# First mixer: the second group's keys between turning the first head's weights and their use; two splits of weights moved behind the first S5 outputs

## The chip, the cores and the metric

The kernel runs as one program on one core of a Trainium2 chip. The metric is the device time of one execution in microseconds (us); the time before is the median of three executions. The engines are PE (matrix products and transposes), ACT and DVE (elementwise work), POOL (a little elementwise work) and SP (it issues the transfers of weights). Each runs its own list of instructions, and semaphores tie the lists together.

## What is computed

A decoder trunk of two layers on 256 tokens of width 1024, all in float32. Each layer is half a SwiGLU block, a mixer, and half a SwiGLU block. The change lies in the mixer of the first layer, which joins a diagonal state space model (S5) and latent attention (MLA):

```python
def _even_mixer(h, ...):
    u, c_q, c_kv, k_rope = jnp.split(h @ w_in, ...)          # 512, 384, 256, 32 columns
    s5_out = _s5(u, ...)                                     # scan over time, gelu, GLU
    q = (_rmsnorm(c_q, q_norm) @ w_uq)                       # 8 heads of 64 + 32 (rotated)
    kv = (_rmsnorm(c_kv, kv_norm) @ w_ukv)                   # 8 heads: keys of 64, values of 64
    ...
    o = _causal_attention(q_full, k_full, v)                 # 8 heads, 256 x 256, blocks of 128 rows
    return jnp.concatenate([s5_out, o], axis=-1) @ w_out
```

## The kernel before

Every product with weights is made of three products of rounded parts: a piece of float32 weights (128x1024, 512 KB) is loaded into one of five `stage` buffers, ACT casts it into `whi` (L84), and DVE subtracts to get the rest, `wlo` (L85). Cast and subtraction together are a split. After each piece's split the next load is issued on SP's queue (`self.load(1)`), so loads run five pieces ahead of splits. In a mixer the call `more()` splits the next chunk of weights, two pieces as a rule, into a pair of buffers; two such pairs exist, and `queue` holds the chunks that are ready.

In the first mixer MLA's eight heads form two groups of four (g = 0, 1). `queries(g)` (L942) and `keys(g)` (L954) fill `qk`, the queries and keys of four heads; `key_values(g)` (L965) fills `v_sb`. For one head `scores(h)` makes a product `sp` (L1045, L1046), DVE takes the row maxima (L831, two blocks of rows) and ACT the exponentials (L838). `turned` transposes these weights on PE (`pt`, L844), and ACT copies them to `pT` (L846); `values` (L1059 to L1061) multiplies them with `v_sb` into `po`. `attend(h)` turns the weights of head h+1, makes the scores of head h+3, and then the values of head h.

S5 works on two halves (b = 0, 1). `step(b)` lets DVE do the next part of the states of half b: products with cosines and sines, two scans (L990), and then `xs_re` and `xs_im`, each of two multiplications and one subtraction or addition (all through the helper at L144). `outputs(b)` (L1086 to L1088) is 48 PE products per half, eight times two passes each of `tmat`, `xs_re` and `xs_im` into `yp`.

The program is written out by hand as a sequence of such calls at the end of `mixer0`. The tile framework puts the instructions of each engine into an order of its own, near that of the code; each engine then takes its list in that order. Shown in the order of the code, the stretch that matters is:

```python
        queries(1)
        step(0)
        sc[0] = turned(sc[0], pb)
        attend(0)
        step(1)
        keys(1)
        key_values(1)
        attend(1)
        step(1)
        yp = outputs(0)
        attend(2)
```

At the end of `queries(1)` a `more()` splits the output weights `w_out0[2]`, and at the end of `key_values(1)` one splits `w_glu`.

Of the kernel before, what the change touches and what calls it, by code (L numbers as in the profile page):

```python
# [99 lines left out]
def highs_first(ks, whi, wlo, xhi, xlo):  # L100

    ks = list(ks)
    return [(k, w, xhi) for k in ks for w in (whi, wlo)] + [(k, whi, xlo) for k in ks]
# [3 lines left out]
def trunk(ctx: ExitStack, tc: tile.TileContext, x, pos, invf, wff, gains, w_u, w_cq, w_ckv,  # L107
# [16 lines left out]
    def bank(name):  # L124
        return ps.tile([128, 512], F32, tag="bank", name=name)
# [16 lines left out]
    def tt(out, a, b, op):  # L142
        spend(out)
        return nc.vector.tensor_tensor(out=out, in0=a, in1=b, op=op)  # L144
# [696 lines left out]
    def turned(s, pool_):  # L841
        pt = bank("pt")
        for c in range(3):
            nc.tensor.transpose(pt[:, c * 128:(c + 1) * 128], s[:, c * 128:(c + 1) * 128], ident)  # L844
        pT = pool_.tile([128, 384], F32, tag="pT", name="pT")
        nc.scalar.copy(out=pT, in_=pt[:, :384])  # L846
        return pT


    def mixer0(prev):  # L850
# [3 lines left out]
        def more():  # L854
            queue.append(W.pre())
# [76 lines left out]
            for g in range(2):  # L932
                nc.scalar.copy(out=kT[64:, 4 * g:4 * g + 4, :], in_=pt[64:].unsqueeze(1).to_broadcast([64, 4, SEQ]))

        def queries(g, between=None):

            wh, wl = (w[:, :1536].rearrange("p (k h d) -> p k h d", k=3, h=4) for w in queue.pop(0))
            for b in range(2):
                pq = bank("pq").rearrange("p (h c) -> p h c", h=2)
                for j in range(2):  # L940
                    for n, (k, w, a) in enumerate(highs_first(range(3), wh, wl, cqh, cql)):
                        nc.tensor.matmul(pq[:, j], w[:, k, 2 * b + j], a[:, k, :], start=n == 0, stop=n == 8)  # L942
                h = 4 * g + 2 * b
                tt(qT[:, h:h + 2, :], pq, qtab.unsqueeze(1).to_broadcast([128, 2, SEQ]), MUL)
                if b == 0 and between:
                    between()
            more()

        def keys(g):
            wh, wl = (w[:, :1024].rearrange("p (k s c) -> p k s c", k=2, s=2) for w in queue[0])  # L950
            pk = bank("pk").rearrange("p (j c) -> p j c", j=2)
            for j in range(2):
                for n, (k, w, a) in enumerate(highs_first(range(2), wh, wl, ckh, ckl)):
                    nc.tensor.matmul(pk[:, j], w[:, k, 0, 128 * j:128 * j + 128], a[:, k, :], start=n == 0,  # L954
                                     stop=n == 5)
            for r in range(2):
                nc.scalar.copy(out=kT[:64, 4 * g + r:4 * g + 4:2, :], in_=pk[64 * r:64 * r + 64])

        def key_values(g):
            wh, wl = (w[:, :1024].rearrange("p (k s c) -> p k s c", k=2, s=2) for w in queue.pop(0))  # L960
            pv = bank("pv").rearrange("p (t c) -> p t c", t=2)
            for t in range(2):
                sl = slice(t * 128, (t + 1) * 128)
                for n, (k, w, a) in enumerate(highs_first(range(2), wh, wl, ckh, ckl)):
                    nc.tensor.matmul(pv[:, t], a[:, k, sl], w[:, k, 1, :], start=n == 0, stop=n == 5)  # L965
            nc.scalar.copy(out=v_sb[:, :, 256 * g:256 * g + 256], in_=pv)
            more()

        xs_re, xs_im = s4("xs_re", [128, NPAIR, NBLK]), s4("xs_im", [128, NPAIR, NBLK])
        nc.gpsimd.memset(xs_re[:, :, 0:1], 0.0)  # L970
# [40 lines left out]
        def step(b):  # L1011
            next(st[b], None)
# [21 lines left out]
        pb = att.enter_context(tc.tile_pool(name="att2", bufs=2))  # L1034
# [8 lines left out]
        def scores(h):  # L1043
            sp = bank("sp")
            nc.tensor.matmul(sp[:, :128], qT[:, h, :128], kT[:, h, :128], start=True, stop=True)  # L1045
            nc.tensor.matmul(sp[:, 128:384], qT[:, h, 128:], kT[:, h, :], start=True, stop=True)  # L1046
            s = pa.tile([128, 384], F32, tag="s", name="s")
            mx = small("mx2", 2)
            row_maxima(sp, s, 96 ** -0.5, mx)
            row_exps(s, mx, lsum[:, 2 * h:2 * h + 2])  # L1050
            return s

        def values(h, pT):
            g, k = divmod(h, 4)
            if k == 0:
                po[g] = bank("po").rearrange("p (t h d) -> p t h d", t=2, h=4)
            o = po[g]
            v = slice(64 * h, 64 * h + 64)
            nc.tensor.matmul(o[:, 0, k, :], pT[:, :128], v_sb[:, 0, v], start=True, stop=True)  # L1059
            nc.tensor.matmul(o[:, 1, k, :], pT[:, 128:256], v_sb[:, 0, v], start=True, stop=False)  # L1060
            nc.tensor.matmul(o[:, 1, k, :], pT[:, 256:384], v_sb[:, 1, v], start=False, stop=True)  # L1061
# [20 lines left out]
        def outputs(b):  # L1082
            yp = bank("yp").rearrange("p (q n) -> p q n", q=8)
            for q in range(8):
                k = 8 * b + q
                nc.tensor.matmul(yp[:, q, :], tmat[:, k, :], u[:, k, :], start=True, stop=False)  # L1086
                nc.tensor.matmul(yp[:, q, :], w_re[:, k, :], xs_re[:, k, :], start=False, stop=False)
                nc.tensor.matmul(yp[:, q, :], w_im[:, k, :], xs_im[:, k, :], start=False, stop=True)  # L1088
            return yp
# [50 lines left out]
        sc = {}  # L1140

        def attend(h):
            if h < 7:
                sc[h + 1] = turned(sc[h + 1], pb)
            if h < 5:
                sc[h + 3] = scores(h + 3)
            values(h, sc.pop(h))

        queries(0, keys_turned)
        step(1)  # L1150
        keys(0)
        step(0)
        key_values(0)
        for h in range(3):
            sc[h] = scores(h)
        step(1)
        step(0)
        queries(1)
        step(0)
        sc[0] = turned(sc[0], pb)  # L1160
        attend(0)
        step(1)
        keys(1)
        key_values(1)
        attend(1)
        step(1)
        yp = outputs(0)
        attend(2)
        step(1)
        attend(3)  # L1170
        osb = normalised(0)
# [261 lines left out]
    state = (lambda: None, [], None, 1.0, [], 1)  # L1433
    state = ffn(state, gains[0], setup())
    state = mixer0(state)
    state = ffn(state, gains[1])
    state = ffn(state, gains[2])
# [4 lines left out]
    g = [gt[:, :512], gt[:, 512:]]  # L1442
# [105 lines left out]
```

## Time and profile before

| what | value |
|---|---|
| time, median of 3 (lowest to highest) | 1006.1 us (1005.62 to 1006.48) |
| the profiled execution: its own time, its span | 1006.91 us, 1005.1 us |
| busy share of the span: PE, DVE, ACT, POOL | 98%, 66%, 56%, 3% |
| the first mixer in the span | about 212 to 320 us |
| the stretch that the change touches | about 264 to 287 us |

The span is what the profiler recorded between the first and the last instruction; the execution's own time has 1.8 us more around it. PE's busy share says that it nearly always has a product in flight, not that it is at its peak. Times in the rows below are counted from the start of the span; rows merge neighbouring equal instructions, and a note in square brackets gives the idle time just before a row and what ended it.

### The profile page before, as it was taken

How to read it: one execution, taken by the hardware profiler on the slowest of the kernel's cores; microseconds unless marked ns; L12 is line 12 of the kernel's file. 1: busy time of each engine (PE TensorE's matmuls, PEld its weight loads, DVE VectorE, ACT ScalarE, POOL GpSimd, SP SyncE). 2: the span in 40 equal slices, each digit the busy share in tenths (PEclk: the TensorE clock that was granted, in tenths of full speed). 3: DMA queues.
4: the chain of work that ended last, by engine and by line, in shares of the span. 5: the costliest groups of instructions: out<-in, count | busy, mean ns of one | idle time of the engine just before them, and what ended most of it. 6: DMA issues, size and time to landing. Idle time of an engine off the chain costs nothing.

```text
span 1005.1 us, 14729 instructions
## 1 busy us (share of the span) xinstructions
PE 986.0 (98%) x5546; PEld 848.3 (84%) x5546; DVE 666.8 (66%) x1223; ACT 567.7 (56%) x1025; POOL 33.5 (3%) x56
## 2 busy tenths in 40 slices
PE   8999999989999999999999999999999999999996
PEld 6888899869988888888898888888888788888885
DVE  6888863867977955555577555555567687555543
ACT  6665654645665845555466555544567676555542
POOL 3100000001000000000000000000001100000000
PEclk9999999999999999999999999999999999999999
DMA  8856554415315865555537555561644447555511
GB/s 289 282 187 189 189 168 145 150 60 157 124 38 176 304 220 189 188 188 189 168 127 261 184 189 187 190 212 54 209 158 136 147 167 268 196 188 190 191 59 42
DMA packets 49801, 174.80 MB, mean 174 GB/s; under 512 B 6081, under 2 KB 7361, under 8 KB 49730
## 3 DMA queue, kind: packets, MB, share of 16 engines
q1 hardware_dynamic: 48576, 170.33, 52.2%
q10 hardware_dynamic: 1154, 3.54, 1.1%
q8 instruction: 43, 0.70, 0.3%
q14 instruction: 28, 0.23, 0.1%
HBM read 172.80 MB, written 1.05 MB: 173 GB/s over the span
## 4 chain that ended last, share of the span: by engine, by line
PE 79%; DVE 7%; DMA 5%; ACT 5%; issue 3%; POOL 0%; POOLq 0%; DVEq 0%; SPq 0%; ACTq 0%
PE gu L333 25%; PE acc L366 21%; PE gu L335 13%; PE proj L813 6%; DMA stage<-in_wff_dram 5%; PE acc L824 3%; DVE wlo L85 3%; ACT whi L84 1%; PE pu L813 1%; PE gt L386 1%; PE cq L813 1%; PE pt L221 1%; PE pq L942 1%; PE ckv L813 1%; ACT dhi L84 1%
## 5 line engine op out<-in xcount | busy, mean ns | idle before, releaser
L333 PE MATMUL gu<-y,whi 128*128 128x512 f32 x1216 | 432.9, 398 | 0.0
L85 DVE TENSOR_TENSOR wlo<-stage,whi 128x1024 fp32r<-128x1024 f32 (+3 forms) x244 | 282.2, 1169 | 190.0 <-ACT whi L84 189.6
L335 PE MATMUL gu<-y,wlo 128*128 128x256 f32 x1216 | 341.4, 281 | 0.4 <-DVE wlo L85 0.4
L84 ACT CAST whi<-stage 128x1024 fp32r<-128x1024 f32 (+3 forms) x244 | 241.9, 1007 | 111.9 <-PE gu L333 71.2
L333 PEld LDWEIGHTS gu<-y,whi 128*128 128x128 f32 x1216 | 228.5, 188 | 55.5
L335 PEld LDWEIGHTS gu<-y,wlo 128*128 128x128 f32 x1216 | 229.7, 189 | 3.3 <-DVE wlo L85 0.7
L366 PE MATMUL acc<-dhi,hs 128*128 128x512 f32 x704 | 192.8, 392 | 1.8 <-ACT hs L155 1.3
L366 PEld LDWEIGHTS acc<-dhi,hs 128*128 128x128 f32 x704 | 126.3, 188 | 29.5 <-DVE hs L144 1.9
L85 DVE TENSOR_TENSOR dlo<-stage,dhi 128x1024 fp32r<-128x1024 f32 x88 | 107.1, 1218 | 32.0 <-ACT dhi L84 31.9
L84 ACT CAST dhi<-stage 128x1024 fp32r<-128x1024 f32 x88 | 92.3, 1050 | 40.4 <-DMA stage<-in_wff_dram 40.2
L366 PE MATMUL acc<-dlo,hs 128*128 128x512 f32 x352 | 110.7, 390 | 0.0
L336 ACT COPY both<-gu 128x256 f32<-128x256 f32 x152 | 56.2, 370 | 76.4 <-PE gu L335 76.1
L144 DVE TENSOR_TENSOR both<-gu,both 128x256 f32<-128x256 f32 x152 | 63.7, 420 | 48.3 <-ACT both L336 48.0
L366 PEld LDWEIGHTS acc<-dlo,hs 128*128 128x128 f32 x352 | 66.1, 188 | 14.3
L155 ACT CAST hs<-sh 128x256 fp32r<-128x256 f32 x80 | 32.5, 407 | 68.8 <-DVE sh L144 68.5
L813 PE MATMUL proj<-whi,y 128*128 128x512 f32 x192 | 62.6, 396 | 0.2 <-ACT y L155 0.2
L339 ACT ACTIVATE sh<-both 128x256 f32<-128x256 f32 x76 | 31.8, 419 | 43.7 <-DVE both L144 43.6
L386 PE MATMUL gt<-whi,y 128*128 128x256 f32 x256 | 50.5, 291 | 0.9 <-ACT y L155 0.7
L386 PEld LDWEIGHTS gt<-whi,y 128*128 128x128 f32 x256 | 41.4, 194 | 2.5 <-ACT y L155 2.5
L813 PEld LDWEIGHTS proj<-whi,y 128*128 128x128 f32 x192 | 36.1, 188 | 8.3 <-ACT y L155 0.5
L144 DVE TENSOR_TENSOR hs<-sh,hs 128x256 fp32r<-128x256 f32 x80 | 33.5, 419 | 6.2 <-ACT hs L155 6.2
L813 PE MATMUL proj<-wlo,y 128*128 128x512 f32 x96 | 37.5, 391 | 0.0
(329 smaller groups left out, 1035.6 us busy)
## 6 DMA issues: line engine op xcount, KB each, us to landing
stage<-in_wff_dram SPq DMA_DIRECT2D x264, 512.0 KB, 4.6
stage<-in_w_in_dram SPq DMA_DIRECT2D x24, 512.0 KB, 4.5
stage<-in_w_out_dram SPq DMA_DIRECT2D x16, 512.0 KB, 3.9
gain<-in_gains_dram ACTq DMA_DIRECT2D x6, 512.0 KB, 4.9
stage<-in_w_u_dram SPq DMA_DIRECT2D x4, 512.0 KB, 4.5
xr<-in_x_dram SPq DMA_DIRECT2D x2, 512.0 KB, 4.6
stage<-in_w_cq_dram SPq DMA_DIRECT2D x2, 512.0 KB, 3.6
stage<-in_w_ckv_dram SPq DMA_DIRECT2D x2, 512.0 KB, 3.4
```

Of the source, the lines that this page charges most:

```text
L84: nc.scalar.copy(out=h, in_=v)
L85: nc.vector.tensor_tensor(out=l, in0=v, in1=h.bitcast(F32), op=ALU.subtract)
L144: return nc.vector.tensor_tensor(out=out, in0=a, in1=b, op=op)
L155: copy = nc.scalar.copy(out=hi, in_=src)
L333: nc.tensor.matmul(gu, gh[:, k, s, :], y2[:, k].rearrange("p s c -> p (s c)"), start=k == 0, stop=False)
L335: nc.tensor.matmul(gu[:, :SEQ], gl[:, k, s, :], yh[:, k, :], start=False, stop=k == KT - 1)
L336: nc.scalar.copy(out=both[:, s], in_=gu[:, SEQ:])
L339: nc.scalar.activation(out=sh[:, 0, :], in_=both[:, 0], func=AF.Silu)
L366: nc.tensor.matmul(acc[t][c], a[:, sl], w[:, c * 512:(c + 1) * 512], start=(f == 0 and n == 0), stop=(f == NF - 1 and n == 2))
L386: last = nc.tensor.matmul(o, a[:, k, sl], w[:, k * 256:(k + 1) * 256], start=(k0 == 0 and n == 0), stop=(k0 > 0 and n == 11))
L813: last = nc.tensor.matmul(acc, a[:, k0 + k, sl], w[:, k * width:(k + 1) * width], start=(k0 == 0 and n == 0), stop=(k0 + per == nk and n = ...
L824: mm = nc.tensor.matmul(acc[t][c], a[:, k0 + k, sl], w[:, o:o + 512], start=(first and k == 0 and n == 0), stop=(last and k == 1 and n == 2))
```

## The change

`keys(1)` moves ahead of `attend(0)`, between the turning of head 0's weights and their use. The last `step(0)` ahead of it moves behind `turned`, and a `step(1)` follows `keys(1)`. The two calls of `more()` that stood at the ends of `queries(1)` and `key_values(1)` come later: one after `outputs(0)`, one after `attend(2)`. No instruction is added or taken away by the code.

```diff
-        def queries(g, between=None):
+        def queries(g, between=None, ahead=True):
...
-            more()
+            if ahead:
+                more()
...
-        def key_values(g):
+        def key_values(g, ahead=True):
...
-            more()
+            if ahead:
+                more()
...
-        queries(1)
+        queries(1, ahead=False)
+        sc[0] = turned(sc[0], pb)
         step(0)
-        sc[0] = turned(sc[0], pb)
+        keys(1)
+        step(1)
         attend(0)
-        step(1)
-        keys(1)
-        key_values(1)
+        key_values(1, ahead=False)
         attend(1)
         step(1)
         yp = outputs(0)
+        more()
         attend(2)
+        more()
```

What the framework makes of it, on three engines. PE's list from the first transposes of attention on (`pt<-ident,s`, three for each head), first before:

```order
L844 MATMUL pt<-ident,s 128x128 x6
L1045 MATMUL sp<-qk 128x128
L1046 MATMUL sp<-qk 128x256
L1059 MATMUL po<-v_sb,pT 128x64
L1060 MATMUL po<-v_sb,pT 128x64
L1061 MATMUL po<-v_sb,pT 128x64
L954 MATMUL pk<-ckh,whi 128x256
```

and after (the lines of the file are shifted by one or two):

```order
L844 MATMUL pt<-ident,s 128x128 x3
L955 MATMUL pk<-ckh,whi 128x256
...
L955 MATMUL pk<-ckl,whi 128x256 x2
L844 MATMUL pt<-ident,s 128x128 x3
L1047 MATMUL sp<-qk 128x128
L1048 MATMUL sp<-qk 128x256
L1061 MATMUL po<-v_sb,pT 128x64
```

Head 0's three transposes are now followed by the twelve products of the second keys (`pk`), and only then come head 1's transposes, the scores of head 3 and the values of head 0.

ACT's list from the last exponentials of head 2 on (`mx_2802` are its row maxima), before:

```order
L838 ACTIVATE s,lsum<-s,mx_2802 128x256
L84 CAST whi<-stage 128x1024 x2
L846 COPY pT<-pt 128x384 x2
L957 COPY qk<-pk 64x2x256 x2
L84 CAST whi<-stage 128x1024
L966 COPY v_sb<-pv 128x2x256
```

and after:

```order
L838 ACTIVATE s,lsum<-s,mx_2802 128x256
L84 CAST whi<-stage 128x1024
L846 COPY pT<-pt 128x384
L84 CAST whi<-stage 128x1024
L958 COPY qk<-pk 64x2x256 x2
L846 COPY pT<-pt 128x384
L967 COPY v_sb<-pv 128x2x256
```

The copy of head 0's turned weights now stands behind one cast of `w_out0[2]` instead of two. The two casts of `w_glu` come later, behind the exponentials of heads 3 and 4.

DVE's list up to the last part of S5's states of half 1, on which `outputs(1)` waits, before (`mx_2988` and `mx_3009` are the row maxima of heads 5 and 6; all four splits of the two chunks stand further ahead):

```order
L144 TENSOR_TENSOR xs_re<-z_re,cosn 128x8x63
L144 TENSOR_TENSOR t_2737<-z_im,sinn 128x8x63
L831 ISA s,mx_2988<-sp,mask 128x128
L831 ISA mx_2988 128x1
L144 TENSOR_TENSOR xs_re<-xs_re,t_2737 128x8x63
L831 ISA s,mx_2988<-sp,mask 128x256
L831 ISA mx_2988 128x1
L144 TENSOR_TENSOR xs_im<-z_im,cosn 128x8x63
L144 TENSOR_TENSOR t_2737<-z_re,sinn 128x8x63
L831 ISA s,mx_3009<-sp,mask 128x128
L831 ISA mx_3009 128x1
L144 TENSOR_TENSOR xs_im<-xs_im,t_2737 128x8x63
```

and after (`mx_2978` are now the row maxima of head 5; the one `wlo` row at the top is the second piece of `w_out0[2]`):

```order
L144 TENSOR_TENSOR xs_re<-xs_re,t_2737 128x8x63
L85 TENSOR_TENSOR wlo<-stage,whi 128x1024
L831 ISA s,mx_2978<-sp,mask 128x128
L831 ISA mx_2978 128x1
L831 ISA s,mx_2978<-sp,mask 128x256
L831 ISA mx_2978 128x1
L85 TENSOR_TENSOR wlo<-stage,whi 128x1024 x2
L144 TENSOR_TENSOR xs_im<-z_im,cosn 128x8x63
L144 TENSOR_TENSOR t_2737<-z_re,sinn 128x8x63
L831 ISA s,mx_3009<-sp,mask 128x128
L831 ISA mx_3009 128x1
L144 TENSOR_TENSOR xs_im<-xs_im,t_2737 128x8x63
```

The two subtractions of `w_glu` now stand between the row maxima of head 5 and the `xs_im` of half 1; before, they stood ahead of those maxima. The subtraction into `xs_re` went the other way, from behind the first maxima to ahead of them.

## Rows read from the trace of the kernel before

**Rows 1.** The page: the chain that ended last, shares by engine.

```profile
PE 79%; DVE 7%; DMA 5%; ACT 5%; issue 3%; POOL 0%; POOLq 0%; DVEq 0%; SPq 0%; ACTq 0%
```

**Rows 2.** PE's waits, 245 to 330 us: total, times, longest.

```profile
PE po L1059 <- ACT pT L846: 0.8, 1, 0.8
PE yp L1088 <- DVE xs_im L144: 0.7, 1, 0.7
```

**Rows 3.** PE in order of time: start, length, instruction, count, idle before.

```profile
263.97 0.82 PE L844 MATMUL pt<-ident,s 128*128 128x128 f32 x6
...
266.27 0.43 PE L1059 MATMUL po<-v_sb,pT 128*128 128x64 f32 x2 [0.83 <-ACT pT L846]
...
266.96 0.37 PE L954 MATMUL pk<-ckh,whi 128*128 128x256 f32 x1
...
268.48 0.28 PE L965 MATMUL pv<-whi,ckh 128*128 128x256 f32 x1
...
269.92 0.49 PE L844 MATMUL pt<-ident,s 128*128 128x128 f32 x3
270.25 0.39 PE L1045 MATMUL sp<-qk 128*128 128x128 f32 x2
...
270.90 0.33 PE L1059 MATMUL po<-v_sb,pT 128*128 128x64 f32 x2
...
271.52 0.39 PE L1086 MATMUL yp<-u,tmat 128*128 128x64 f32 x2
```

**Rows 4.** ACT in order of time, in front of head 0's values.

```profile
263.85 1.99 ACT L84 CAST whi<-stage 128x1024 fp32r<-128x1024 f32 x2 [0.69 <-ACT s L838]
265.75 0.85 ACT L846 COPY pT<-pt 128x384 f32<-128x384 f32 x2
```

**Rows 5.** DVE in order of time, up to the states of half 1.

```profile
272.79 2.33 DVE L85 TENSOR_TENSOR wlo<-stage,whi 128x1024 fp32r<-128x1024 f32 x2
275.05 0.28 DVE L831 CUSTOM_DVE_ANT_0 s<-sp,mask 128x128 f32<-128x128 f32 x1
...
275.60 0.68 DVE L144 TENSOR_TENSOR xs_re<-z_re,cosn 128x504 f32<-128x504 f32 x1
276.20 0.67 DVE L144 TENSOR_TENSOR t<-z_im,sinn 128x504 f32<-128x504 f32 x1
278.07 0.29 DVE L831 CUSTOM_DVE_ANT_0 s<-sp,mask 128x128 f32<-128x128 f32 x1 [1.21 <-PE sp L1046]
...
278.29 0.68 DVE L144 TENSOR_TENSOR xs_re<-xs_re,t 128x504 f32<-128x504 f32 x1
...
280.62 0.68 DVE L144 TENSOR_TENSOR xs_im<-xs_im,t 128x504 f32<-128x504 f32 x1
```

**Rows 6.** PE in order of time, from the end of the first S5 outputs.

```profile
276.88 0.50 PE L844 MATMUL pt<-ident,s 128*128 128x128 f32 x3
277.21 0.39 PE L1045 MATMUL sp<-qk 128*128 128x128 f32 x2
...
280.15 0.33 PE L1086 MATMUL yp<-u,tmat 128*128 128x64 f32 x2
...
281.36 0.43 PE L1088 MATMUL yp<-xs_im,w_im 128*128 128x64 f32 x2 [0.65 <-DVE xs_im L144]
...
286.32 0.61 PE L1077 MATMUL pt<-ident,osb 128*128 128x128 f32 x4
```

**Rows 7.** The page's DMA issues: count, size, median us to landing.

```profile
stage<-in_w_out_dram SPq DMA_DIRECT2D x16, 512.0 KB, 3.9
```

**Rows 8.** ACT in order of time: the first cast of the later loads.

```profile
298.44 1.05 ACT L84 CAST whi<-stage 128x1024 fp32r<-128x1024 f32 x1
```

**Rows 9.** The page: PE's granted clock in 40 slices, in tenths.

```profile
PEclk9999999999999999999999999999999999999999
```

**Rows 10.** PE in order of time: eight transposes after idle time.

```profile
7.55 1.97 PE L221 MATMUL pt<-ident,y 128*128 128x128 f32 x8 [1.46 <-DVE y L148]
...
212.93 1.23 PE L221 MATMUL pt<-ident,y 128*128 128x128 f32 x8 [1.65 <-DVE y L148]
```

## The prediction

> **What bounds the kernel now.** I read the page's chain first: PE holds 79% of it, and no other engine more than 7% [rows 1]. So a change inside a mixer is worth what it does to PE's idle time, and I turned to PE's waits. Over the second half of the first mixer and the start of the block behind it there are only two of note: the values of head 0 wait 0.83 us for ACT's copy `pT`, and `outputs(1)` waits 0.65 us for the last operation into `xs_im` [rows 2, 3, 6]. Together 1.48 us, or 0.15% of the time: more than that the change can hardly win. What a measurement of this kernel can tell from no change is about 0.2%, or 2.0 us.
>
> PE, ACT and DVE in order of time then show who is late. Head 0's copy stands behind two casts, which ran for 1.99 us from 263.85 [rows 4]; the transposes that it copies had started at 263.97 [rows 3]. DVE is the second late engine: it stood idle for 1.21 us until the scores of head 5 were there, and took their row maxima at 278.07. The operation into `xs_re` at 278.29 followed only then, though both of its inputs had been written before the wait [rows 5]: what stands behind a waiting instruction in DVE's list waits with it. `xs_im` ended at 280.62 + 0.68 = 281.30, and PE went on at 281.36 [rows 5, 6].
>
> **The first wait goes.** From starts in PE's rows I take three transposes at 270.25 - 269.92 = 0.33, scores of a head 0.65, values of a head 0.62, the second keys 268.48 - 266.96 = 1.52, and the second values 269.92 - 268.48 = 1.44 [rows 3]. In the new order PE does transposes, keys, transposes and scores from 263.97 on, so it comes to head 0's values at 263.97 + 0.33 + 1.52 + 0.33 + 0.65 = 266.80. ACT now has one cast ahead of the copy: 263.85 + 1.99/2 + 0.85/2 puts the copy's end near 265.3 [rows 4]. The wait goes, with 1.5 us to spare; the second cast, which stands behind the copy now, could last more than twice as long as it does before anything of head 0 noticed. Then values, second values, transposes, scores and values: 266.80 + 0.62 + 1.44 + 0.33 + 0.65 + 0.62 = 270.46 for the start of `outputs(0)`, against 271.52 [rows 3]. That is a gain of 1.06: the idle time and some slow starts around it. The second keys end at 265.82, and the scores that read them come at 269.19, so ACT's copies of the keys have 3.4 us.
>
> **The second wait grows.** DVE has the same work to do up to `xs_im` before and after; only its place against the wait for head 5's scores differs. The scores come earlier by PE's gain: 5.36 us of `outputs(0)` and three transposes are unchanged in front of them [rows 3, 6], so the row maxima can start at 278.07 - 1.06 = 277.01. Before, DVE came to that wait at 278.07 - 1.21 = 276.86. Now the two subtractions of `w_glu`, 275.05 - 272.79 = 2.26 together, are no longer in front of it, and one operation of `xs_re`, 276.20 - 275.60 = 0.60, is [rows 5]. So it comes at 276.86 - 2.26 + 0.60 = 275.20 and stands idle for 1.81 us. Behind the wait there were 281.30 - 278.07 = 3.23 us of work up to the end of `xs_im`; now there are 3.23 + 2.26 - 0.60 = 4.89. `xs_im` ends at 277.01 + 4.89 = 281.90, and PE goes on 0.06 later, at 281.96 instead of 281.36 [rows 6]. PE itself would have come to these products at 281.36 - 0.65 - 1.06 = 279.65: its wait grows from 0.65 to 2.31.
>
> So the change takes 1.06 us out at head 0 and puts 1.66 us in at `outputs(1)`: **0.60 us slower**. Queued behind PE's waiting product are the rest of `outputs(1)`, the heads' transposes at 286.32 [rows 6], and everything after them; ACT's and DVE's gelu of half 1 waits for the same products. All of it moves by 0.60.
>
> **What else moves, at nothing.** The casts of `w_glu` must end before DVE wants them at 277.01 plus the maxima. They may start when the maxima of head 4 have been used, and those end three operations of 0.60 and two subtractions of 1.13 before 275.20, at 271.14 [rows 5]: nearly 6 us for exponentials and two casts of 1.99 [rows 4]. If that cover were gone, each microsecond lost there would be a microsecond at `xs_im`. Four loads of 512 KB move with the four splits, the last to about 280; such a load lands 3.9 us after its issue, and the cast of the first of them comes at 298.44 [rows 7, 8], 14 us later. The order of SP's queue is the same. The split chunks themselves are used only behind the transposes at 286.32 [rows 6]. From there on no order changes that matters.
>
> **The rivals.** *No payback.* DVE would not be late, because head 5's scores came earlier than I have them. With the maxima free to start at once, at 275.20, `xs_im` ends at 280.09 and PE goes on at 280.15: 1.21 us faster, 1004.9. It would be no loss from a start of 276.41 on. For it speaks that PE has lost its other wait; against it that the scores stand behind 5.36 us of `outputs(0)` in PE's own list [rows 3, 6], and nothing that I can see pulls them 0.6 us forward. If DVE let the subtractions pass while it waits, the result would be the same 1.21; the `xs_re` row speaks against that [rows 5].
>
> *The delay is absorbed.* If a later stage waits for something that this change doesn't move, the 0.60 disappears there: 1006.1. Transfers are 5% of the chain [rows 1], so there are places where loads are late. But the loads behind the mixer are issued when splits free their buffers, and those splits wait for products that shift with PE.
>
> [...]
>
> **How the numbers follow.** The profiled execution took 1006.91, 0.8 above the median of three, which alone says how far single executions lie apart. The step is added to the median: 1006.1 + 0.6 = 1006.7. The forecast has a chance of 0.76, with a range of its own from 1006.0 to 1007.5: DVE's arithmetic is good to some 0.3 us, and a median of three to about as much. No payback has 0.10, absorption 0.08, the lower clock 0.06. The range from 1005.2 to 1008.0 holds the forecast and absorption and leaves no payback in full (1004.9) and the lower clock out, 0.16 together. Slower by over 0.2% (above 1008.1) is the lower clock and a tail of the forecast, 0.07; faster by over 0.2% (below 1004.1) would need more than both waits, 0.02; the rest, 0.91, lies within.
>
> **What would show it.** In the profile of the changed kernel PE's wait for `pT` at head 0 should be gone and `outputs(0)` should start about 1 us sooner after the first transposes. DVE should stand idle for about 1.8 us ahead of head 5's row maxima, with the two subtractions of `w_glu` right behind them. PE's wait for `xs_im` should be about 2.3 us, with the products behind it at the same distance from each other as before. I am wrong if that wait is below 1.7, if a new wait stands ahead of `outputs(0)`, or if the products behind the gap are farther apart.

## The result, and the profile after

The changed kernel takes 1012.93 us (median of six runs, 1011.63 to 1013.69) against 1005.5 (1005.06 to 1006.48) for the kernel before on the same chip: an estimated ratio of 1.0062, interval 1.0047 to 1.0077 (the two medians by themselves stand 1.0074 apart). By the medians it is slower by 7.4 us where I forecast 0.6, and above my range. The profiled execution took 1012.7 us, its span is 1010.9 against 1005.1, and its mean granted clock is 0.992 against 0.998.

First the page's line of PE's granted clock in tenths, in 40 slices of 25 us, to be held against [rows 9]; then PE's waits in the stretch of [rows 2].

```profile
PEclk9999999999979999999999999999999999999999
```

```profile
PE yp L1090 <- DVE xs_im L144: 2.3, 1, 2.3
```

One slice of the 40 is not at nine tenths: the twelfth, around 290 us. The wait for `pT` is gone, and the wait for `xs_im` is the 2.3 us that were forecast. PE in order of time shows both, and what came behind the second wait (start, length, instruction, count, idle before):

```profile
262.80 0.49 PE L844 MATMUL pt<-ident,s 128*128 128x128 f32 x3
...
265.54 0.33 PE L1061 MATMUL po<-v_sb,pT 128*128 128x64 f32 x2
...
269.23 0.39 PE L1088 MATMUL yp<-u,tmat 128*128 128x64 f32 x2
...
278.03 0.39 PE L1089 MATMUL yp<-xs_re,w_re 128*128 128x64 f32 x2
280.75 0.69 PE L1090 MATMUL yp<-xs_im,w_im 128*128 128x64 f32 x2 [2.33 <-DVE xs_im L144]
281.23 0.63 PE L1088 MATMUL yp<-u,tmat 128*128 128x64 f32 x2
281.65 0.64 PE L1089 MATMUL yp<-xs_re,w_re 128*128 128x64 f32 x2
...
289.76 0.63 PE L1090 MATMUL yp<-xs_im,w_im 128*128 128x64 f32 x2
290.19 1.06 PE L1079 MATMUL pt<-ident,osb 128*128 128x128 f32 x4
...
294.10 0.72 PE L824 MATMUL acc<-whi,oh 128*128 128x512 f32 x2
```

From the waiting product to the heads' transposes PE now takes 290.19 - 280.75 = 9.44 us, before 4.96 [rows 6]: the products stand (289.76 - 281.65)/19 = 0.427 us apart, a pair each, and PE waits for nobody between them. In the kernel before the same twenty pairs stand (286.09 - 281.85)/19 = 0.223 us apart, and the first `acc` product, which comes behind the heads' transposes, starts at 288.33:

```profile
281.85 0.39 PE L1087 MATMUL yp<-xs_re,w_re 128*128 128x64 f32 x2
...
286.09 0.39 PE L1088 MATMUL yp<-xs_im,w_im 128*128 128x64 f32 x2
...
288.33 0.71 PE L824 MATMUL acc<-whi,oh 128*128 128x512 f32 x2
```

The windows of the changed kernel say why (busy time of each engine, then the granted clock, the share of the DMA engines and GB/s):

```profile
278.00:280.00 2.00, 0.41 (x4) 0.28 (x3) 2.00 (x4) 0.15 (x2) 0.00 (x0) 1.00 0.66 231
280.00:281.00 1.00, 0.25 (x1) 0.25 (x2) 1.00 (x6) 0.49 (x2) 0.00 (x0) 0.74 0.82 242
281.00:285.00 4.00, 4.00 (x20) 4.00 (x21) 2.29 (x7) 2.20 (x5) 0.00 (x0) 0.50 0.24 91
285.00:290.00 5.00, 5.00 (x26) 5.00 (x26) 0.00 (x0) 0.00 (x0) 0.00 (x0) 0.50 0.00 0
290.00:294.00 4.00, 4.00 (x19) 3.82 (x18) 1.49 (x6) 2.61 (x7) 0.00 (x0) 0.50 0.01 4
294.00:295.00 1.00, 1.00 (x6) 0.87 (x6) 0.65 (x2) 1.00 (x4) 0.00 (x0) 0.93 0.00 0
```

Towards the end of the wait the clock goes from 1.00 to 0.50, and it stays there until shortly after 294, for more than 13 us. The sum for this execution, against the rows of before: from head 0's transposes to the waiting product 280.75 - 262.80 = 17.95 us, before 281.36 - 263.97 = 17.39 [rows 3, 6], a loss of 0.56. From the waiting product to the first `acc` product at 294.10 it is 13.35 us; the same work took 288.33 - 281.36 = 6.97 before, a loss of 6.38. Together 6.94; this execution had come to head 0's transposes 1.17 sooner, which leaves 5.8, the difference of the spans. From the first `acc` product to the end both executions take 716.8 us, so nothing behind it gave any of this back.

### The profile page after: what moved, and what is told of

Read it like the earlier page. It is cut to its first block, busy times and chain, and to the rows that moved or that the text cites. A ratio compares the mean times of both kernels' runs of the same rounds, so it can differ in the third digit from the quotient of the medians.

```text
span 1010.9 us, 14731 instructions
## 1 busy us (share of the span) xinstructions
PE 992.2 (98%) x5546; PEld 855.8 (85%) x5546; DVE 667.3 (66%) x1223; ACT 567.4 (56%) x1025; POOL 34.0 (3%) x56
## 4 chain that ended last, share of the span: by engine, by line
PE 89%; DVE 4%; DMA 3%; ACT 2%; issue 1%; POOL 0%; SPq 0%; POOLq 0%; DVEq 0%; ACTq 0%
PE gu L333 27%; PE acc L366 23%; PE gu L335 13%; PE proj L813 6%; PE acc L824 4%; PE gt L386 3%; PE gu L349 2%; DMA stage<-in_wff_dram 2%; DVE wlo L85 1%; PE pu L813 1%; PE pq L942 1%; PE cq L813 1%; PE pt L221 1%; DMA xr<-in_x_dram 1%; PE ckv L813 1%
```

## The experiments

**Theory A**: a wait of PE of this length at this place lowers its clock, and the rest of the mixer pays. **Theory B**: the slow stretch comes from the new order itself, by something other than the wait. A ratio is against the kernel before, timed beside it on the same chip. "Fallen" counts the runs with a mean granted clock of 0.995 or less: 7 us at 0.50 lower the mean by 0.0035 from 0.998. The mean says how long the clock was low and not where, and only one run of each kernel has a profile. The last 3.9 us of the span are at 0.50 too in the profile of before, the last 3.4 in those of the changed kernel and of number 1, behind PE's last product; in a run of 1005 us that is 0.002 of the mean. I take a mean of 0.997 to 0.999 as undisturbed, and a difference of 0.001 says nothing.

| kernel | PE's wait at the second outputs, us | median, us | ratio (interval) | fallen |
|---|---|---|---|---|
| before, beside the experiments | 0.65 | 1005.9 to 1006.6 | 1 | 14 of 86 |
| 1, `w_glu` late | none shown | 1005.36 | 0.9993 (0.9984 to 1.0001) | 0 of 11 |
| 2, change and 8 products | 0.5 | 1005.86 | 1.0 (0.9991 to 1.001) | 0 of 11 |
| 3, before with `xs_im` late | 2.19 | 1012.11 | 1.0057 (1.0044 to 1.007) | 6 of 6 |
| 4, keys alone | 0.66 | 1004.76 | 0.9989 (0.9979 to 1.0) | 1 of 12 |
| 5, splits alone | 2.33 | 1011.04 | 1.0052 (1.004 to 1.0064) | 5 of 5 |
| 6, before, `xs_im` later by one | 1.25 | 1010.14 | 1.0041 (1.0029 to 1.0053) | 5 of 5 |
| 7, before and 3 products | none shown | 1005.24 | 0.9996 (0.9986 to 1.0006) | 0 of 12 |
| 8, keys alone and 3 products | 0.2 | 1004.5 | 0.9983 (0.9974 to 0.9992) | 0 of 11 |
| 9, before with a longer gap at 212 us | 0.65 | 1010.27 | 1.0042 (1.003 to 1.0054) | 4 of 5 |
| 10, change and 5 products | 1.18 | 1006.65 | 1.0014 (1.0003 to 1.0024) | 3 of 12 |
| 11, number 9 and 3 products | none shown | 1007.62 | 1.001 (1.0001 to 1.0019) | 0 of 12 |

**1. `w_glu`'s split behind the second outputs.** Only the place of the second `more()` differs from the changed kernel.

```
         yp = outputs(0)
         more()
         attend(2)
-        more()
...
         yp = outputs(1)
+        more()
```

> The changed kernel with the split of w_glu moved once more, behind the call of outputs(1): DVE has nothing but S5's states behind the row maxima of head 5. Theory A (the wait of 2.33 us for xs_im is what lowers PE's clock): the wait shrinks to about 0.1 us, the clock stays at its upper level, and the time falls below that of the kernel before by both of its waits, 1005.5 - 1.06 - 0.6 = about 1003.8 us. Theory B (the new order itself lowers it, by the run of small products and transposes that now stands in front of outputs(1), whatever the wait): the clock falls all the same, about 1003.8 + 6.4 = 1010.2 us.

The wait and the fall are gone, and the time is not told from that of before. The further gain that A expected was not there: a new wait of PE took it, since ACT's copy for a later head now stood behind five activations of the gelu (PE's waits, then ACT in order of time):

```profile
PE po L1061 <- ACT pT L846: 1.2, 1, 1.2
```

```profile
288.77 3.33 ACT L1111 ACTIVATE gt<-gs 32x256 f32<-32x256 f32 x5 [0.76 <-DVE gs L148]
292.13 0.48 ACT L846 COPY pT<-pt 128x384 f32<-128x384 f32 x1
```

This wait of 1.21 us, at 292.66, has no fall behind it: the profile shows a granted clock of 1.00 from 276 to 302, and none of the 11 runs is below 0.997.

**2. The changed kernel with its wait filled.** Products into a bank that nobody reads stand in front of the second outputs; order and splits are the change's.

```
+        junk = bank("junk")
+        fill = cqh.rearrange("p k c -> p (k c)")
+        for n in range(8):
+            nc.tensor.matmul(junk, fill[:, :128], fill[:, :512], start=n == 0, stop=n == 7)
         yp = outputs(1)
```

> The changed kernel with eight more products of 512 columns in front of outputs(1), about 1.9 us of work whose result nobody reads; DVE is as late as before. Theory A: PE stands idle for some 0.5 us only, the clock stays up, and although work was added the time falls from 1012.9 to 1005.5 + 0.6 = about 1006.1 us. Theory B: everything in front of and behind the gap is as it was, so about 1012.9 us.

PE still comes to the rest of `outputs(1)` when `xs_im` is there, as late as in the change, and yet the 7 us are gone. That speaks against B: the order is the same. The products do two things, they shorten the wait and they give PE more work; number 1 shortened the wait without them.

**3. The kernel before with `xs_im` late.** The first multiplication of `xs_im` b1 is done three times.

```
-                tt(xs[:, h, o], x[:, :, a], c[:, :, a], MUL)
+                for _ in range(3 if b == 1 and xs is xs_im else 1):
+                    tt(xs[:, h, o], x[:, :, a], c[:, :, a], MUL)
```

> The kernel before with the first multiplication into xs_im of half 1 done three times instead of once (the same numbers are written again), so that DVE is 1.2 to 1.5 us later at the point on which outputs(1) waits; nothing is reordered on PE. Theory A: the wait grows from 0.65 to about 2.1 us, the clock falls behind it, 1005.5 + 1.5 + 6.4 = about 1013.4 us. Theory B: the order on PE is that of before, the clock stays up, about 1007.0 us.

The old order with a wait of 2.19 us shows nearly the whole loss, 6.1 us by the medians. The waiting product and the windows:

```profile
280.80 0.43 PE L1089 MATMUL yp<-xs_im,w_im 128*128 128x64 f32 x2 [2.19 <-DVE xs_im L144]
```


```profile
278.00:281.00 3.00, 0.81 (x8) 0.68 (x6) 2.96 (x10) 2.56 (x10) 0.00 (x0) 1.00 0.01 3
281.00:282.00 1.00, 1.00 (x7) 1.00 (x7) 0.86 (x3) 0.75 (x2) 0.00 (x0) 0.55 0.00 0
...
290.00:295.00 5.00, 5.00 (x21) 4.68 (x21) 2.14 (x7) 3.77 (x9) 0.00 (x0) 0.52 0.02 3
295.00:300.00 5.00, 5.00 (x32) 4.35 (x32) 4.83 (x12) 3.59 (x6) 0.00 (x0) 1.00 0.00 0
```

**4 and 5. The two parts of the change apart.** Number 4 has the new place of the second keys and leaves both splits where they were; number 5 the reverse.

```
# 4: the keys alone
         queries(1)
+        sc[0] = turned(sc[0], pb)
         step(0)
-        sc[0] = turned(sc[0], pb)
-        attend(0)
-        step(1)
         keys(1)
+        step(1)
+        attend(0)
# 5: the splits alone
-        queries(1)
+        queries(1, ahead=False)
...
-        key_values(1)
+        key_values(1, ahead=False)
...
         yp = outputs(0)
+        more()
         attend(2)
+        more()
```

> The keys and the steps moved as in the change, both splits left where they were before. The wait for head 0's copy goes (1.06 us), the wait for xs_im stays near 0.65 us. Theory A: the clock stays up, 1005.5 - 1.06 = about 1004.4 us. Theory B: the clock falls as in the changed kernel, about 1010.8 us.

> The kernel before with only the second half of the change: both splits of weights stand behind S5's first outputs, the second keys stay where they were. Theory A (the splits alone make the long wait, and a wait of that length is what lowers TensorE's clock): the wait for xs_im b1 at the second outputs is 2.0 to 2.5 us, the granted clock in the ten us behind it about 0.5, the median 1011 to 1013.5. Rival (the long wait needs the new place of the second keys too, since that takes away the wait of 0.8 us ahead of it): a wait under 1.5 us, the clock kept at 1.00 in most runs, the median 1005 to 1007.

The splits alone make the wait of 2.33 us and most of the loss; the keys alone make none of it. One of the twelve runs of number 4, the profiled one, took 1007.37, and there a wait of 0.66 had a fall of 7 us behind it:

```profile
278.67 0.43 PE L1090 MATMUL yp<-xs_im,w_im 128*128 128x64 f32 x2 [0.66 <-DVE xs_im L144]
```

```profile
281.00:282.00 1.00, 1.00 (x7) 1.00 (x7) 0.63 (x1) 0.33 (x1) 0.00 (x0) 0.59 0.00 0
...
285.00:288.00 3.00, 3.00 (x15) 3.00 (x16) 0.43 (x1) 1.52 (x3) 0.00 (x0) 0.50 0.00 0
288.00:290.00 2.00, 2.00 (x13) 1.76 (x13) 1.63 (x7) 1.77 (x7) 0.00 (x0) 1.00 0.03 8
```

So the wait of 0.65 that the kernel before has always had might lower its clock now and then. Numbers 6 to 8 ask that.

**6. A wait in between.** As number 3, with `range(2 ...)`: the multiplication done twice.

> The kernel before with the first multiplication of xs_im b1 done twice (the second time with the same result), which lengthens PE's wait at the second outputs by one multiplication: two more of them had taken it from 0.65 to 2.19 us, so one gives about 1.4. If the fall of the clock is a matter of chance that grows with the wait, some runs fall and some don't: times between 1005.5 and 1012 in two groups, a median between 1006 and 1010. If only waits near 2 us or more do it, no run is over 1009 and the median is 1006.5 to 1007. If every wait over one us does it, all runs are over 1010.

All five runs fell by their mean clock, though two of them (1008.86 and 1009.0) stay under the 1010 that every run should have passed. In the profiled one the clock is low for 6.8 us, against 10.2 to 13.7 behind the waits of 2.19 to 2.33 us:

```profile
279.93 0.43 PE L1089 MATMUL yp<-xs_im,w_im 128*128 128x64 f32 x2 [1.25 <-DVE xs_im L144]
```


```profile
280.00:282.00 2.00, 2.00 (x19) 2.00 (x19) 1.23 (x6) 1.70 (x6) 0.00 (x0) 1.00 0.02 4
282.00:284.00 2.00, 2.00 (x14) 2.00 (x13) 1.24 (x2) 0.63 (x1) 0.00 (x0) 0.62 0.00 0
...
288.00:290.00 2.00, 2.00 (x13) 1.94 (x11) 0.90 (x2) 1.56 (x3) 0.00 (x0) 0.67 0.00 0
290.00:292.00 2.00, 2.00 (x14) 1.66 (x14) 1.44 (x7) 1.62 (x5) 0.00 (x0) 1.00 0.03 8
```

The fall comes some 2.6 us behind the end of the wait.

**7 and 8. The small wait filled.** Three such products as in number 2 (`range(3)`), once in the kernel before, once in number 4.

> The kernel before with three products of 512 columns that nobody reads in front of the second outputs (about 0.64 us, as long as the wait of 0.65 us that stands there). If the few of its runs with a mean clock of 0.996 or less (5 of 29, four of them over 1007) come from that wait, the wait is under 0.2 us, no run has a mean clock under 0.997, the highest time is under 1007.2 and the median 1005 to 1006. If they come from elsewhere, about two of eleven runs still have them.

> The second keys moved as in the change, both splits left where they were, and three products of 512 columns that nobody reads in front of the second outputs. Theory A: the wait of 0.66 us at the second outputs is filled, no run has a mean clock under 0.997, the highest time is under 1006.5, the median 1004 to 1005 (the kernel with the keys alone had 1004.8 and one run of 1007.4 at 0.995), so it is the quickest of all by some 0.1% over the kernel before. Rival (the occasional fall doesn't hang on that wait): about one run in ten at 1007 or more, and the median not under 1004.8.

The count of before that number 7 names is too low: of its 29 runs then, four were at 0.995 or less and eight at 0.996 or less. Two signs that number 7 named failed: two of its runs are at 0.996, and they took 1008.5 and 1008.22, which stays unexplained; its median is not told from that of before. By 0.995 none of the 23 runs with the wait filled fell, against 15 of 98 with it (14 of 86 of before, one of 12 of number 4); chance alone would give none of 23 about one time in thirty, so that the wait has a share in these falls is likely and not shown. Number 8 is the quickest kernel of all, and the only one whose interval lies below 1, but its gain over number 4 by the products is not told from none. In its profile the wait is short and the clock stays up:

```profile
PE yp L1090 <- DVE xs_im L144: 0.2, 1, 0.2
```

```profile
278.00:283.00 5.00, 5.00 (x43) 4.78 (x41) 3.18 (x11) 3.83 (x12) 0.00 (x0) 1.00 0.01 2
```

**9. A long gap at another place.** `normed` gets an argument that only the first mixer sets, and writes the first half of `y` for the first 128 rows of the sequence twice.

```
-            last = stt(y[:, sl], xr[t][:, sl], rs, g[c], MUL, MUL).ins
+            for _ in range(2 if late and c == 0 else 1):
+                last = stt(y[:, sl], xr[t][:, sl], rs, g[c], MUL, MUL).ins
```

> The kernel before, with the longest gap of PE inside it made as long as the one that lowers the clock: ahead of the first mixer's first eight transposes (212.93 us in the profile, a wait of 1.65 us that showed a granted clock of 1.00 behind it in all ten profiles so far) the operation into y that PE waits for is done twice with the same result, one more operation of about 0.69 us. The gap should be about 2.3 us. Theory A1 (the length of a gap alone decides): the clock falls to about 0.5 behind it for 6 us or more in every run, the median 1010 to 1014. Theory A2 (the length alone doesn't decide, it hangs on the place too): the clock stays at 1.00, the time rises by the 0.7 us of the operation alone, the median 1006 to 1007.5.

The gap became 2.95 us, longer than meant, so that 2.3 us at this place were not tried; at 2.95 the clock does fall here too:

```profile
212.22 1.89 PE L221 MATMUL pt<-ident,y 128*128 128x128 f32 x8 [2.95 <-DVE y L148]
```

```profile
208.00:212.00 4.00, 1.27 (x6) 0.72 (x4) 3.79 (x7) 2.41 (x8) 0.56 (x1) 1.00 0.00 0
212.00:213.00 1.00, 0.78 (x4) 0.81 (x5) 0.07 (x1) 0.00 (x0) 0.00 (x0) 0.65 0.00 0
213.00:215.00 2.00, 2.00 (x9) 1.59 (x8) 0.93 (x2) 1.42 (x3) 0.00 (x0) 0.50 0.00 0
215.00:216.00 1.00, 1.00 (x5) 0.80 (x4) 0.58 (x2) 1.00 (x1) 0.34 (x1) 0.65 0.00 0
216.00:220.00 4.00, 4.00 (x23) 3.39 (x22) 2.55 (x4) 1.31 (x4) 0.21 (x1) 1.00 0.00 0
...
284.00:286.00 2.00, 2.00 (x12) 2.00 (x11) 1.24 (x2) 0.63 (x1) 0.00 (x0) 0.50 0.00 0
```

But it is back after 3.4 us, where A1 had 6 or more. The median is in A1's range for another reason: the larger part of the loss comes with a second fall, from 284 us on, behind the old wait of 0.65 (291.82 - 281.58 = 10.24 us from the waiting product to the first `acc` product, before 6.97).

**10. The changed kernel with half of its wait left.** As number 2 with five products.

> The changed kernel with five products of 512 columns that nobody reads in front of the second outputs instead of eight, so that a wait of 2.33 - (5 x 0.213) = 1.27 us is left there, and no wait for pT at head 0 stands ahead of it (in the kernel with a wait of 1.25 us such a wait of 0.8 stood 14 us earlier). If the wait at the second outputs decides by itself, the clock falls in every run and the median is 1009 to 1011. If it needed the earlier wait as well, no run falls and the median is 1006.

Neither: 3 of 12 runs fell, and the profiled one did not (1.00 in all windows from 275 to 295). That is not told from the kernel before (2 of 17 beside it, 14 of 86 in all), so it is not shown that a wait of 1.18 us lowered the clock here; 1.25 did in number 6, in each run. The two kernels differ in the earlier wait for `pT`, in the five products and in 0.07 us; which of these matters was not told apart. Unless those 0.07 us decide, the length of the wait is not all that counts. The five products took 2.33 - 1.18 = 1.15 us off the wait, 0.23 each, where the expectation's 0.213 was an estimate.

**11. Number 9 with the wait of 0.65 filled.** Three products, as in number 7.

> The kernel of the run before last (the first mixer's y written twice, a gap of 2.95 us at 212 us with 3 us at 0.50 behind it) with three products of 512 columns that nobody reads in front of the second outputs, which fill the wait of 0.65 us there. In the profile without them the clock fell a second time, from 284 us on, behind that wait, and the mean clock of four of five runs was 0.993, more than 3 us at 0.50 make. If the second fall hangs on the wait, filling it leaves the first fall alone: mean clock 0.996 to 0.997 in all runs, a median of 1007 to 1008.5. If it comes from the fall at 212 us and not from that wait, the mean clock stays at 0.993 in most runs and the median at 1009.5 to 1010.5.

No run is below 0.996, and the profile shows 1.00 from 275 to 290: the second fall hung on the wait at the second outputs. What the gap at 212 us costs is read from the traces of numbers 9 and 7: it is 2.95 - 1.63 = 1.3 us longer in number 9 (in number 11 2.96), and from its transposes to the last row of five products into `pu` number 9 takes 223.07 - 212.22 = 10.85 us, number 7 220.69 - 210.77 = 9.92, so 3.4 us at 0.50 cost 0.9. For number 11 the ratios give 1.001 - 0.9996 = 0.0014, or 1.4 us, with an uncertainty about as large.

## Why the prediction was wrong

**The waits were right.** `outputs(0)` starts 269.23 - 262.80 = 6.43 us behind head 0's transposes; from 263.97 to 270.46 I had 6.49. DVE's idle time ahead of head 5's row maxima is 1.76 us (forecast 1.81), with the two subtractions of `w_glu` right behind them, as these rows of DVE say:

```profile
275.78 0.29 DVE L831 CUSTOM_DVE_ANT_0 s<-sp,mask 128x128 f32<-128x128 f32 x1 [1.76 <-PE sp L1048]
...
276.35 2.36 DVE L85 TENSOR_TENSOR wlo<-stage,whi 128x1024 fp32r<-128x1024 f32 x2
...
280.01 0.68 DVE L144 TENSOR_TENSOR xs_im<-xs_im,t 128x504 f32<-128x504 f32 x1
```

PE's wait is 2.33 (forecast 2.31), and the sum of these steps is 0.56 (forecast 0.60). Number 5 adds that the splits alone make the second wait, and that they alone take the first away too; so do the keys alone, in number 4.

**What failed is the step "All of it moves by 0.60", which has the work behind the wait keep its pace, and with it what I gave the lower clock: a chance of 0.06 and a price of 3.0 us.** The products behind the wait did not keep "the same distance from each other as before" (0.427 us against 0.223), the last of my three signs of being wrong, and that cost 6.38 us where the forecast had nothing. The chance was that low because of one row: a gap of 1.65 us at 212.93, behind which nothing fell [rows 10]. That row stands at another place, and it could only say that 1.65 was harmless there, not that 2.31 would be. At 212 us all eight gaps of 1.62 to 1.66 us in the profiles of experiments 1 to 8 have 1.00 behind them, and so has the wait of 1.21 us at 292.66 in number 1. At the second outputs 1.25 us lowered the clock in all of five runs and 2.2 to 2.3 in all of 17 (the changed kernel, numbers 3 and 5), by their mean clocks and by the four profiles. That a gap lowers the clock only above 1.65 us was my estimate from that row; it is wrong for this place by at least 0.4 us, and the row of a gap without a fall spoke for no other place. In the changed kernel the clock then stayed at 0.50 for 13 us in which PE was busy all the time (4.00, 5.00 and 4.00 us of the windows from 281 to 294), so that PE's return to work did not end the price.

**The price was mis-sized in both factors.** I took 4.96 us of work, the rest of `outputs(1)` [rows 6], times 0.6, from the 1.97 us of eight transposes against 1.23, a factor of 1.6 [rows 10]. No run shows the 3.0 us of this estimate; the changed kernel shows 6.38. The lower level lasted past that work, through transposes, scores and values to 294.10, 6.97 us of work at the old pace; and the factor is 13.35/6.97 = 1.92, close to the 2 between the two levels. The eight transposes of 1.97 us stand at the program's start, where the trace gives a granted clock of 1.00, so by that record the row did not show the lower level; and eight transposes behind a gap are a poor measure of it, since at 0.50 in number 9 they took 1.89, only 1.54 times the 1.23. The price is 6.4 us and not 3.0, and with it a fall of the clock stood at 1006.7 + 6.4 = 1013.1. That the median is 1012.9 is in part luck: the kernel before took 1005.5 beside it and not 1006.1, so the sum is 0.5 short of the 7.4 measured. The mean clocks of the six runs go from 0.989 to 0.992, the profiled one's, so some of the others were slowed for longer than it was.

The rivals *no payback* and *the delay is absorbed* fall with the rows above: DVE did wait, and the 0.56 us are there to the end.

**What stays open**: why gaps of 1.65 and 1.21 us are harmless at other places and 1.25 is not at the second outputs; why 0.65 us there is mostly harmless (at most 14 of 86) but not behind the fall at 212 us (4 of 5); and why the clock was back after 3 us in one place and after 7, 10 or 14 in the other.

## What to carry to other kernels

Price a new wait of TensorE twice: by its length, and by the work behind it at the lower clock, which meant half the pace in the changed kernel (0.427 us against 0.223) and lasted 3.4 to 13.7 us in these runs; here 1.7 us more of waiting brought 6.4 us of slower work behind it. A gap elsewhere in the trace without a fall behind it is no evidence for another place. Runs of one program whose mean granted clock differs by more than its end explains (here 0.994 to 0.999) are a reason to look for a wait that sometimes lowers it. Work for which nobody waits belongs behind the operation that TensorE waits for, not in front of it (with `w_glu`'s split there the wait of 2.33 us was gone in number 1); and where a wait of some 2 us can't be removed, products that nobody reads in its place can be worth their time, as the eight of number 2, which took the 7 us back. For the wait of 0.65 us the gain of three is not told from none.

## What the runs showed of the hardware

- The fall is not tied to the end of the wait. By the windows it came some 0.3 us before the end in the changed kernel (0.74 between 280 and 281), 0.3 us after it in number 3 (0.55 between 281 and 282), 1.1 us after it in number 5 (0.54 between 281 and 282, the wait of 2.33 us over at 280.02), and about 2.5 us after it behind the shorter waits of numbers 4, 6 and 9 (0.59 between 281 and 282, 0.74 between 282 and 283, 0.74 between 283 and 285), when PE had long been at work again.
- Read in steps of 1 or 2 us, the lower level lasted 13.7 us behind the waits of the changed kernel and number 3 and 10.2 behind that of number 5, 6.8 behind shorter ones at the same place (numbers 4, 6 and 9), and 3.4 behind 2.95 us at 212 us. PE was at work all through these stretches, but for the first 0.3 us in the changed kernel.
- A wait can lower the clock at one place and a longer one leave it alone at another: 1.25 us at the second outputs had a fall behind it in all of five runs, 1.65 us ahead of the transposes at 212 us had none, nor had 1.33 us at 207.59 in the kernel before or 1.21 us at the values of a later head in number 1.
- In the first 12 us of the kernel before the granted clock reads 1.00, yet products of 256 columns (`gt`) stand 0.21 us apart up to 11.2 us and 0.12 from 12.6 on. Whether that is the lower level, which the record then misses, no run shows.
- Three products of 512 columns more, with no other change on TensorE, left no run at 0.995 or less in 23, where 15 of 98 without them were; two of the 23 at 0.996 stay unexplained.
